# Two-level transfers for split blocks, doubled raw blocks, and biases asked for ahead, in a two-layer encoder

## The chip, the cores and the metric

The kernel runs on one core of a Trainium2 chip. The metric is the device time of one execution in microseconds (us); the median of several runs counts, and a profiled execution gives the trace. The engines are named as in the profile: PE (TensorE), DVE (VectorE), ACT (ScalarE), POOL (GpSimd) and SP (SyncE). SP, ACT and POOL issue transfers (DMAs), which 16 DMA engines of the core carry out.

## What is computed

Two layers of an encoder over 512 tokens of width 1024. Each has a feed-forward step, a mixer and a second feed-forward step; the mixer is what this case is about. The reference, cut to it:

```python
def reference(x, ...):
    for l in range(DEPTH):
        y = swiglu(rmsnorm(h, ffn1_pre_g[l]), ffn1_w_gu[l], ffn1_w_down[l])
        h = h + 0.5 * rmsnorm(y, ffn1_post_g[l])
        u = rmsnorm(h, mix_pre_g[l])
        proj = u @ w_in[l]
        qa, ka, va, qb, kb, vb, qc, kc, vc, gl = jnp.split(proj, split_at, axis=-1)
        oa = neighbourhood_attention(split_heads(qa, 8), split_heads(ka, 8), split_heads(va, 8), na_rpb[l])
        ob = sliding_window_attention(apply_rope(split_heads(qb, 8), cos, sin),
                                      apply_rope(split_heads(kb, 2), cos, sin),
                                      split_heads(vb, 2), sw_sink[l])
        ...   # qc, kc are turned by apply_rope too; two softmax maps per head
        oc = differential_attention(qc, kc, vc, lam, lam_init, diff_subln_g[l])
        ...
        yb = jnp.einsum('bsnc,ncd->bsnd', branches, w_branch[l])
        gates = jax.nn.sigmoid(gl.reshape(b, s, 3, D_MODEL) + b_gate[l])
        h = h + rmsnorm(jnp.sum(gates * yb, axis=2) @ w_out[l], mix_post_g[l])
        ...   # second feed-forward step

def apply_rope(t, cos, sin):
    t1, t2 = jnp.split(t, 2, axis=-1)
    return t * cos + jnp.concatenate([-t2, t1], axis=-1) * sin
```

The neighbourhood attention adds a bias to the scores, which is gathered from a small table `rpb` for each of 8 heads.

## The kernel before, in words

Every product is made of single-precision operands that are split in a high part `hi` and the rest `lo`, so that several fast matmuls give the exact product. A block is a tile of 128 rows (channels) and 512 columns (tokens), 262 KB.

**Projection** (`project`, one phase per layer). Column blocks of the projection (QA, KA, VA, QB, KB, VB, QC, KC, VC, then the gates from GL on) come out of PE, are evicted by ACT, and go to memory (DRAM) by POOL's queue. Blocks of queries and keys of branches A and B are split in `hi` and `lo` by `stacked` and stored as two tiles "part" by `store` (L1405). Blocks of QC and KC are stored as they are, as "raw", also by L1405; they are turned by the rotary step later, in the mixer.

**Mixer** (`mixer`). The string ORDER names its pieces in the order in which the code writes them: `qa`, `aa` (queries, keys, values of a pair of heads of branch A, and their attention), `kb`, `qb`, `ab` (branch B), `qc`, `ac`, `fc` (branch C), `ga` to `gc` (gates, 24 matmuls each, which fill PE between the attentions), `ya` to `yc` (the branches' output matmuls). A scheduler then orders each engine's instructions by its own costs, and each engine works its list strictly in order.

What a pair of heads needs is loaded by SP's queue. A *stack* `st` has 128 rows: 64 rows of `hi` over 64 rows of `lo` of the same head (or `lo` over `hi`), so that one matmul takes both. `restacked` fills each with two transfers of 64 rows (L1783, L1784) from the two "part" tiles. Blocks QA and KA (the first pair) stay on the chip. So the other three pairs of branch A load 6 stacks each (2 of the query block, 4 of the key block), and branch B loads 12: 30 stacks per layer. There are 14 buffers for them.

`rope` loads a raw block `x` (L1760) and a copy `sh` with its 32-row quarters exchanged in pairs (four transfers, L1768), and DVE then multiplies `x` by a table (L1769), `sh` by another (L1770) and adds (L1771). There are 8 such blocks per layer.

`ask` loads a head's raw biases `braw` (L1729) and has DVE form an edge tile and a middle tile `bedge`, `bmid` from them (L1744), in buffers of tag "g" (10 of them). `qkv_a` loads a pair's stacks and values first, and then asks for that pair's own biases.

The transfers of SP and ACT share eight completion semaphores in turn: a transfer that is given a semaphore waits, in its queue, until the one before it on that semaphore has landed.

Where a load's source is not a plain block, its access pattern is written out as a list of [pitch, count], outermost first. Before, that is so for the biases alone:

```python
    def raw_of(l, hd):
        return bass.AP(rpb.tensor, (l * 8 + hd) * 16 * RPBW, [[RPBW, 8], [1, 16], [1, 8 * RPBW]])
```

This is 8 runs of 16 rows of 512 numbers, laid into 128 rows of the tile.

Of the kernel before, what the change touches and what calls it, by code (L numbers as in the profile page):

```python
# [10 lines left out]
F32 = mybir.dt.float32  # L11
# [5 lines left out]
P = 128  # L17
# [3 lines left out]
T = 512  # L21
# [18 lines left out]
QA, KA, VA, QB, KB, VB, QC, KC, VC, GL = 0, 4, 8, 12, 16, 17, 18, 22, 26, 30  # L40
# [79 lines left out]
def encoder_kernel(ctx: ExitStack, tc: tile.TileContext, order, xT, wts, cols, rows, rpb, consts, tables, out):  # L120
    nc = tc.nc
# [5 lines left out]
    dr = ctx.enter_context(tc.tile_pool(name="dr", bufs=1, space=bass.MemoryType.DRAM))  # L127
# [19 lines left out]
    def nm(s):  # L147
        serial[0] += 1
        return f"{s}{serial[0]}"

    def big(tag, dt=F32, shape=(P, T), name="v"):
        if tag in BUFS:
            return sb.tile(list(shape), dt, tag=tag, name=nm(name), bufs=BUFS[tag])
        kind, pool = phase[0]
        return pool.tile(list(shape), dt, tag=tag, name=nm(name), bufs=ABUFS[kind][tag])
# [7 lines left out]
    V, A, G, PE = nc.vector, nc.scalar, nc.gpsimd, nc.tensor  # L163

    def f(t):
        return t.bitcast(F32)
# [94 lines left out]
    for l in range(L):  # L261
        for which in (1, 2):
            name = f"ffn{which}_w_down"
# [1104 lines left out]
    def project(l, op, accs):  # L1368
# [34 lines left out]
        def store(kind, x):  # L1403
            d = dr.tile([P, T], F32, tag=kind, name=nm(kind), bufs=60)
            G.dma_start(d, f(x))  # L1405
            return d

        def parts(x):
            hi, lo = big("t", F32R, name="hi"), big("t", F32R, name="lo")
            A.activation(hi, x, AF.Copy)  # L1410
            V.tensor_tensor(out=lo, in0=x, in1=f(hi), op=ALU.subtract)
            return hi, lo

        def stacked(c, x):
            hi, lo = parts(x)
            if c in (QA, KA):
                made[c] = []
                for s in range(2):
                    own, res = slice(64 * s, 64 * s + 64), []
                    for one, two in ((hi, lo), (lo, hi))[: 1 if c == QA else 2]:  # L1420
                        st = slots.pop(0)
                        nc.sync.dma_start(f(st)[0:64], f(one)[own])
                        nc.sync.dma_start(f(st)[64:128], f(two)[own])
                        res.append(st)
                    made[c].append((res + [None])[:2])
                return
            made[c] = store("part", hi), store("part", lo)

        def turned(c, x, heads):
            tp = bank("at")  # L1430
# [13 lines left out]
        turning, slowly, values = [], [], []  # L1444
# [5 lines left out]
        def turned_by(c, x):  # L1450
            sh = big("t", name="sh")
            for q in range(4):
                o = q ^ 1
                nc.sync.dma_start(sh[32 * q : 32 * q + 32], x[32 * o : 32 * o + 32])
            slowly.extend(
                (
                    lambda: V.tensor_tensor(out=x, in0=x, in1=turning[0], op=ALU.mult),
                    lambda: V.tensor_tensor(out=sh, in0=sh, in1=turning[1], op=ALU.mult),
                    lambda: V.tensor_tensor(out=x, in0=x, in1=sh, op=ALU.add),
                    lambda: stacked(c, x),  # L1460
                )
            )

        def ready(c, x):
            if c >= GL:
                gated(c, x)
            elif c < VA:
                stacked(c, x)
            elif QB <= c < VB:
                turned_by(c, x)  # L1470
            elif c < KB or c >= VB and (c < QC or c >= VC):
                values.append(lambda: turned(c, x, 1 if c >= VC else 2))
            else:
                made[c] = store("raw", x)

        def now():
            while values:
# [2 lines left out]
        def out(c, acc):  # L1480
            x = big("t", name="x")
            evict(x, c, acc)
            ready(c, x)
            now()

        made = {}
# [38 lines left out]
        for n, c0 in (("cosR", 0), ("sinR", 512)):  # L1525
            t = big("rr", name=n)
# [25 lines left out]
        def tables_of_a():  # L1552
            t = sb.tile([P, 4, T], F32, tag="n", name=nm("pre"), bufs=BUFS["n"])
            nc.sync.dma_start(t[:, 0, :], tables[:, 1024 : 1024 + 512])
            nc.sync.dma_start(t[:, 1, :256], tables[:, 1024 + 512 : 1024 + 768])
            for hd in range(2):
                nc.sync.dma_start(t[:, 2 + hd, :], raw_of(l, hd))
            made["tables"] = t
            made["edges"] = sb.tile([P, 4, T], F32, tag="n", name=nm("edges"), bufs=BUFS["n"])

        def gated(c, t):
            d = made["gates"][divmod(c - GL, KD)] = dr.tile([P, T], F32, tag="gate", name=nm("gate"), bufs=4 * KD)
            G.dma_start(d, t)
# [71 lines left out]
        work(len(slowly))  # L1635
        return made

    def raw_of(l, hd):
        return bass.AP(rpb.tensor, (l * 8 + hd) * 16 * RPBW, [[RPBW, 8], [1, 16], [1, 8 * RPBW]])

# [76 lines left out]
    def mixer(l, op, made):  # L1717
# [3 lines left out]
        for n in range(3):  # L1721
            masks[n] = pre[:, n // 2, 256 * (n % 2) : 256 * (n % 2) + 256]

        def ask(hd):
            if hd < 2:
                raws[hd] = pre[:, 2 + hd, :]
                return
            raw = raws[hd] = big("g", name="braw")
            nc.sync.dma_start(raw, raw_of(l, hd))  # L1729

        def biases(hd):
            raw = raws.pop(hd)
            if hd < 2:
                edge = made["edges"][:, hd, :]
                mid = made["edges"][:, 2, 2 * P * hd : 2 * P * (hd + 1)]
            else:
                edge = big("g", name="bedge")
                mid = big("g", shape=(P, 2 * P), name="bmid")

            def put(dst, mask, n0, n1):  # L1740

                src = raw[:, 7 * RPBW + 39 - 8 * n0 :]
                (ps0, pn), _ = src.ap
                V.tensor_tensor(  # L1744
                    out=dst.rearrange("p (d r c) -> p d r c", r=8, c=8),
                    in0=bass.AP(src.tensor, src.offset, [[ps0, pn], [-8, n1 - n0], [-RPBW, 8], [-1, 8]]),
                    in1=mask.rearrange("p (d r c) -> p d r c", r=8, c=8),
                    op=ALU.add,
                )

            put(edge[:, 0:256], masks[0], 0, 4)
            put(mid, masks[1], 0, 4)
            put(edge[:, 256:384], masks[2][:, :P], 2, 4)
            put(edge[:, 384:512], masks[2][:, P:], 0, 2)
            return lambda i: edge[:, 0:256] if i == 0 else edge[:, 256:512] if i == NT - 1 else mid


        def load(d, dt=F32, tag="tx"):
            x = big(tag, dt, name="x")
            nc.sync.dma_start(f(x), d)  # L1760
            return x

        def rope(c):
            x = load(made[c])
            sh = big("tx", name="sh")
            for q in range(4):
                o = q ^ 1
                nc.sync.dma_start(sh[32 * q : 32 * q + 32], made[c][32 * o : 32 * o + 32])  # L1768
            V.tensor_tensor(out=x, in0=x, in1=turning[0], op=ALU.mult)  # L1769
            V.tensor_tensor(out=sh, in0=sh, in1=turning[1], op=ALU.mult)  # L1770
            V.tensor_tensor(out=x, in0=x, in1=sh, op=ALU.add)  # L1771
            return x

        def restacked(c, both):
            if c in (QA, KA):
                return made[c]
            hi, lo = made[c]
            res = []
            for s in range(2):
                own, pair_ = slice(64 * s, 64 * s + 64), []  # L1780
                for one, two in ((hi, lo), (lo, hi))[: 2 if both else 1]:
                    st = big("st", F32R, name="st")
                    nc.sync.dma_start(f(st)[0:64], one[own])  # L1783
                    nc.sync.dma_start(f(st)[64:128], two[own])  # L1784
                    pair_.append(st)
                res.append((pair_ + [None])[:2])
            return res

        def values(c):
            t = made[c] if c == VA else [load(d, F32R, "st") for d in made[c]]  # L1790
            if c >= VC:
                return t
            v = [x.rearrange("p (b h d) -> p b h d", b=2, h=2) for x in t]
            return lambda j, s: v[j // 2][:, j % 2, s, :]
# [11 lines left out]


        def qkv_a(p):
            got = restacked(QA + p, False), restacked(KA + p, True), values(VA + p)
            for s in range(2):  # L1810
                ask(2 * p + s)
            return got

        oa = [sb.tile([P, 4, T], F32R, tag="X", name=nm("oa"), bufs=BUFS["X"]) for _ in range(2)]

# [121 lines left out]
        def qkv_b(c):  # L1937
            return restacked(c, c == KB)
# [69 lines left out]
        at = len(order) // HB  # L2008
# [62 lines left out]
    for l in range(L):  # L2071
        with open_phase("f"):
            X, accs = ffn(l, 1, X, accs)
        with open_phase("p"):
            made = project(l, X, accs)
# [63 lines left out]
```

## Time and profile before

| | |
|---|---|
| median of 3 runs | 2371.69 us (2371.62 to 2374.82) |
| profiled execution | 2370.88 us |
| its span, first to last instruction | 2369.1 us |
| mean granted PE clock | 0.996 |
| PE busy | 2342.6 us, 99% |
| DVE / ACT / POOL busy | 1892.4 / 1446.8 / 223.8 us |
| moved by DMA | 395.16 MB, mean 167 GB/s |
| stack loads `st<-part`, both layers | 120 of 128 KB |

The profile is read by views: the page with its table of engines; the waits, which give for each line the tile waited for, who made it, us in total, times, and the longest; the windows, which give for a stretch its length, then the busy time (and the instructions) of PE, PE's weight loads, DVE, ACT and POOL, then the granted PE clock as a share, the mean busy share of the 16 DMA engines, and GB/s; the timeline, with start, duration, engine, line, operation, tiles (out<-in), and in brackets the idle time before and what ended it; and the list of DMA issues, with count, KB each and the median us from issue to landing. Packets are the pieces in which the DMA engines move data; the profile counts them by size.

### The profile page before, as it was taken

Reading aid. Unit: us, or ns where it says so; the run is one execution under the profiler, and the core shown is the slowest. Engines: PE = TensorE matmul, PEld = TensorE weight load, DVE = VectorE, ACT = ScalarE, POOL = GpSimd, SP = SyncE. Lnnn points to the kernel's source line nnn. Section 1 sums busy time; section 2 is a strip of 40 time slices with the busy share of each in tenths; the row PEclk is TensorE's granted clock in tenths of the full one; section 3 lists DMA queues with packets and bytes.
Section 4 is the critical chain, followed back from the end, with each engine's and each line's share of the span. In section 5 each row is a group of like instructions: output and inputs, shape, how many; then the busy total and the mean of one; then the engine's idle time right before and its main releaser. Section 6 shows DMA issues by size and latency. Waiting matters only on the chain. (4 is left out here: it accounts for less than half of the span.)

```text
span 2369.1 us, 40269 instructions
## 1 busy us (share of the span) xinstructions
PE 2342.6 (99%) x15134; PEld 2109.5 (89%) x15134; DVE 1892.4 (80%) x3082; ACT 1446.8 (61%) x2715; POOL 223.8 (9%) x354
## 2 busy tenths in 40 slices
PE   9999999999999999999999999999999999999998
PEld 8999889997888889998899998889978788899987
DVE  7887988966888668888878878889579876788796
ACT  6555566667777465655655554666687764556563
POOL 0111001110121001110001110011101200011100
PEclk9999999999999999999999999999999999999999
DMA  5566446667565524664525565276774664256642
GB/s 170 162 169 190 154 145 187 207 219 207 168 174 189 167 97 147 166 162 165 175 87 168 162 178 196 102 216 199 222 206 139 195 206 140 97 147 172 190 148 84
DMA packets 138147, 395.16 MB, mean 167 GB/s; under 512 B 19296, under 2 KB 26080, under 8 KB 137440
## 3 DMA queue, kind: packets, MB, share of 16 engines
q1 hardware_dynamic: 102960, 260.37, 35.0%
q0 software_dynamic: 20160, 78.66, 12.4%
q10 hardware_dynamic: 14832, 53.56, 7.4%
q8 instruction: 119, 1.95, 0.3%
q14 instruction: 76, 0.62, 0.1%
HBM read 326.98 MB, written 80.74 MB: 172 GB/s over the span
## 5 line engine op out<-in xcount | busy, mean ns | idle before, releaser
L680 PE MATMUL mm<-X,h 128*128 128x256 f32 x1504 | 268.0, 278 | 1.2 <-DVE v L738 1.2
L680 PEld LDWEIGHTS mm<-X,h 128*128 128x128 f32 x1504 | 228.5, 188 | 2.5 <-DVE v L738 2.0
L225 DVE TENSOR_TENSOR w<-wr,w 128x512 fp32r<-128x512 f32 x264 | 178.9, 685 | 56.2 <-ACT w L224 55.2
L224 ACT ACTIVATE w<-wr 128x512 fp32r<-128x512 f32 x264 | 162.5, 627 | 96.4 <-PE mm L328 40.8
L326 PE MATMUL mm<-X,w 128*128 128x512 f32 (+1 forms) x570 | 218.3, 383 | 1.8 <-ACT X L553 1.8
L328 PE MATMUL mm<-X,w 128*128 128x512 f32 (+1 forms) x570 | 216.4, 380 | 0.8 <-DVE w L225 0.8
L327 PE MATMUL mm<-X,w 128*128 128x512 f32 (+1 forms) x570 | 216.2, 379 | 0.8 <-DVE X L554 0.7
L680 PE MATMUL mm<-ht,h 128*128 128x256 f32 x752 | 210.1, 279 | 0.0
L680 PE MATMUL mm<-ht,l 128*128 128x256 f32 x752 | 210.1, 279 | 0.0
L680 PE MATMUL mm<-lt,h 128*128 128x256 f32 x752 | 209.4, 278 | 0.0
L680 PE MATMUL mx<-ht,h 128*128 128x256 f32 x752 | 208.3, 277 | 0.6 <-ACT v L724 0.6
L680 PE MATMUL mm<-X,l 128*128 128x256 f32 x752 | 208.2, 277 | 0.0
L680 PE MATMUL mx<-ht,l 128*128 128x256 f32 x752 | 208.1, 277 | 0.0
L680 PE MATMUL mx<-lt,h 128*128 128x256 f32 x752 | 207.9, 277 | 0.0
L630 DVE TENSOR_TENSOR l<-wr,h 128x1024 fp32r<-128x1024 f32 x94 | 114.9, 1222 | 65.7 <-PE mm L680 65.7
L662 ACT ACTIVATE h<-wr 128x1024 fp32r<-128x1024 f32 x94 | 99.9, 1062 | 78.7 <-PE mx L680 55.5
L680 PE MATMUL at<-X,w 128*128 128x256 f32 x1128 | 144.2, 277 | 0.0
L680 PEld LDWEIGHTS mx<-ht,h 128*128 128x128 f32 x752 | 141.2, 188 | 1.4 <-ACT v L724 1.4
L680 PEld LDWEIGHTS mm<-ht,l 128*128 128x128 f32 x752 | 141.7, 188 | 0.1
L680 PEld LDWEIGHTS mm<-ht,h 128*128 128x128 f32 x752 | 141.7, 188 | 0.0
L680 PEld LDWEIGHTS mm<-lt,h 128*128 128x128 f32 x752 | 141.7, 188 | 0.0
L680 PEld LDWEIGHTS mx<-ht,l 128*128 128x128 f32 x752 | 141.2, 188 | 0.2 <-DVE l L640 0.2
(458 smaller groups left out, 6802.4 us busy)
## 6 DMA issues: line engine op xcount, KB each, us to landing
wr<-in_wts_dram SPq DMA_DIRECT2D x273, 512.0 KB, 4.6
wr<-in_wts_dram ACTq DMA_DIRECT2D x102, 512.0 KB, 4.1
sum<-in_wts_dram POOLq DMA_DIRECT2D x64, 512.0 KB, 5.3
st<-part SPq DMA_DIRECT2D x120, 128.0 KB, 5.1
ap<-in_wts_dram SPq DMA_DIRECT2D x20, 512.0 KB, 5.6
a<-kept SPq DMA_DIRECT2D x32, 256.0 KB, 6.3
ap<-sum SPq DMA_DIRECT2D x16, 512.0 KB, 4.3
x<-part SPq DMA_DIRECT2D x32, 256.0 KB, 3.8
```

The source lines that it names most:

```text
L224: A.activation(hi, raw, AF.Copy)
L225: V.tensor_tensor(out=lo, in0=raw, in1=f(hi), op=ALU.subtract)
L326: PE.matmul(acc, w[0], x[0], start=start, stop=False)
L327: PE.matmul(acc, w[0], x[1], start=False, stop=False)
L328: PE.matmul(acc, w[1], x[0], start=False, stop=stop)
L630: V.tensor_tensor(out=w["l1"], in0=self.raws[g][0], in1=f(w["h1"]), op=ALU.subtract)
L662: A.activation(self.W[g]["h24"], self.raws[g][1], AF.Copy)
L680: PE.matmul(acc, ws[i], xs[j], start=start and k == m == 0, stop=stop and k == n - 1 and m == 2, skip_group_check=True,)
```

## The change

Four edits, all in `project` and `mixer`, the same in both layers.

1. `stacked` stores `hi` and `lo` into one DRAM tile "both", one under the other, for key blocks whose stacks are needed in both orders `hi` once more as a third part. `restacked` loads each stack with one transfer instead of two.
2. A raw block is stored twice, by two transfers, so that its tile holds the upper 64 rows twice and then the lower 64 rows twice.
3. `rope` loads `x` from it, and the exchanged copy `sh` in one transfer instead of four.
4. `qkv_a` asks for biases ahead of its stacks: heads 0 to 3 with the first pair, 4 and 5 with the second, 6 and 7 with the third. The middle tiles of two heads share one buffer.

The function `halves(d, row)` names 64 rows from `row` and 64 rows from `row + 128` of a tile; as an access pattern that is 2 runs of 64 rows of 512 numbers.

```diff
--- before.py
+++ after.py
@@ -1424,7 +1424,11 @@
                         res.append(st)
                     made[c].append((res + [None])[:2])
                 return
-            made[c] = store("part", hi), store("part", lo)
+            n = 2 + (KA <= c < VA or c == KB)
+            d = dr.tile([n * P, T], F32, tag=f"both{n}", name=nm("both"), bufs=60)
+            for at, t in enumerate((hi, lo, hi)[:n]):
+                G.dma_start(d[P * at : P * at + P], f(t))
+            made[c] = d
 
         def turned(c, x, heads):
             tp = bank("at")
@@ -1471,7 +1475,9 @@
             elif c < KB or c >= VB and (c < QC or c >= VC):
                 values.append(lambda: turned(c, x, 1 if c >= VC else 2))
             else:
-                made[c] = store("raw", x)
+                made[c] = dr.tile([2 * P, T], F32, tag="raw", name=nm("raw"), bufs=60)
+                for n in range(2):
+                    G.dma_start(halves(made[c], 64 * n), f(x))
 
         def now():
             while values:
@@ -1635,6 +1641,10 @@
         work(len(slowly))
         return made
 
+    def halves(d, row):
+        pitch = d.ap[0][0]
+        return bass.AP(d.tensor, d.offset + row * pitch, [[P * pitch, 2], [pitch, 64], [1, T]])
+
     def raw_of(l, hd):
         return bass.AP(rpb.tensor, (l * 8 + hd) * 16 * RPBW, [[RPBW, 8], [1, 16], [1, 8 * RPBW]])
 
@@ -1721,6 +1731,8 @@
         for n in range(3):
             masks[n] = pre[:, n // 2, 256 * (n % 2) : 256 * (n % 2) + 256]
 
+        mids = []
+
         def ask(hd):
             if hd < 2:
                 raws[hd] = pre[:, 2 + hd, :]
@@ -1735,7 +1747,9 @@
                 mid = made["edges"][:, 2, 2 * P * hd : 2 * P * (hd + 1)]
             else:
                 edge = big("g", name="bedge")
-                mid = big("g", shape=(P, 2 * P), name="bmid")
+                if hd % 2 == 0:
+                    mids.append(big("g", name="bmid"))
+                mid = mids[-1][:, 2 * P * (hd % 2) : 2 * P * (hd % 2) + 2 * P]
 
             def put(dst, mask, n0, n1):
 
@@ -1761,11 +1775,9 @@
             return x
 
         def rope(c):
-            x = load(made[c])
+            x = load(halves(made[c], 0))
             sh = big("tx", name="sh")
-            for q in range(4):
-                o = q ^ 1
-                nc.sync.dma_start(sh[32 * q : 32 * q + 32], made[c][32 * o : 32 * o + 32])
+            nc.sync.dma_start(sh, halves(made[c], 32))
             V.tensor_tensor(out=x, in0=x, in1=turning[0], op=ALU.mult)
             V.tensor_tensor(out=sh, in0=sh, in1=turning[1], op=ALU.mult)
             V.tensor_tensor(out=x, in0=x, in1=sh, op=ALU.add)
@@ -1774,14 +1786,12 @@
         def restacked(c, both):
             if c in (QA, KA):
                 return made[c]
-            hi, lo = made[c]
             res = []
             for s in range(2):
-                own, pair_ = slice(64 * s, 64 * s + 64), []
-                for one, two in ((hi, lo), (lo, hi))[: 2 if both else 1]:
+                pair_ = []
+                for n in range(2 if both else 1):
                     st = big("st", F32R, name="st")
-                    nc.sync.dma_start(f(st)[0:64], one[own])
-                    nc.sync.dma_start(f(st)[64:128], two[own])
+                    nc.sync.dma_start(f(st), halves(made[c], P * n + 64 * s))
                     pair_.append(st)
                 res.append((pair_ + [None])[:2])
             return res
@@ -1806,10 +1816,9 @@
 
 
         def qkv_a(p):
-            got = restacked(QA + p, False), restacked(KA + p, True), values(VA + p)
-            for s in range(2):
-                ask(2 * p + s)
-            return got
+            for hd in ((0, 1, 2, 3), (4, 5), (6, 7), ())[p]:
+                ask(hd)
+            return restacked(QA + p, False), restacked(KA + p, True), values(VA + p)
 
         oa = [sb.tile([P, 4, T], F32R, tag="X", name=nm("oa"), bufs=BUFS["X"]) for _ in range(2)]
```

The first place in the order is SP's queue at the start of layer 0's mixer, just behind weight loads `wr`. `part` are the two stored parts of a block, `st` a stack, `x<-part` values, `braw` raw biases. Before:

```order
L211 DMA wr_5748<-in_wts_dram 128x1024
L1783 DMA st_5920<-part_4051 64x512
L1784 DMA st_5920<-part_4053 64x512
L1783 DMA st_5923<-part_4051 64x512
L1784 DMA st_5923<-part_4053 64x512
L1783 DMA st_5926<-part_4102 64x512
L1784 DMA st_5926<-part_4104 64x512
L1783 DMA st_5929<-part_4104 64x512
L1784 DMA st_5929<-part_4102 64x512
```

After, where `both` is the new tile:

```order
L211 DMA wr_5749<-in_wts_dram 128x1024
L1741 DMA braw_5921<-in_rpb_dram 128x1x512
L1741 DMA braw_5923<-in_rpb_dram 128x1x512
L1741 DMA braw_5925<-in_rpb_dram 128x1x512
L1741 DMA braw_5927<-in_rpb_dram 128x1x512
L1794 DMA st_5929<-both_4051 128x1x512
L1794 DMA st_5931<-both_4051 128x1x512
L1794 DMA st_5933<-both_4101 128x1x512
L1794 DMA st_5935<-both_4101 128x1x512
L1794 DMA st_5937<-both_4101 128x1x512
L1794 DMA st_5939<-both_4101 128x1x512
L1774 DMA x_5941<-part_4157 128x512
```

The four bias loads stand ahead of the first pair's stacks, and each stack is one row where it was two; a row of a stack now has the same form as a row of a bias load, 128x1x512.

The second place is POOL's queue in layer 0's projection, at the first raw blocks (`raw<-x` and `raw<-v`, from two buffers). Before:

```order
L1405 DMA part_5086<-hi_5082 128x512
L1405 DMA part_5088<-lo_5083 128x512
L1405 DMA raw_5146<-x_5060 128x512
L1405 DMA raw_5151<-v_4991 128x512
L1405 DMA part_5220<-hi_5216 128x512
L1405 DMA part_5222<-lo_5217 128x512
```

After:

```order
L1430 DMA both_5083<-hi_5079 128x512
L1430 DMA both_5083<-lo_5080 128x512
L1480 DMA raw_5142<-x_5057 2x64x512 x2
L1480 DMA raw_5148<-v_4988 2x64x512 x2
L1430 DMA both_5218<-hi_5214 128x512
L1430 DMA both_5218<-lo_5215 128x512
```

Each raw block is stored twice (x2), and its destination is written in 2 runs of 64 rows.

The third place is DVE's list in layer 0's branch A, where the rotary step of the first raw block stands. `bedge` and `bmid` are the bias tiles, `s,nmx` the scores of a head with their bias, `l` the sums of a softmax, `lo` the rest of a split block. Before:

```order
L1678 ISA s_6235,nmx_6234<-mx_6248,bedge_6228 128x256
L1678 ISA nmx_6234 128x1
L225 TENSOR_TENSOR w_6762<-wr_6760,w_6762 128x512
L1769 TENSOR_TENSOR x_7488<-x_7488,cosR_6548 128x512
L1692 RECIPROCAL l_6252<-l_6252 128x4
L353 TENSOR_TENSOR lo_6267<-at_6263,hi_6266 128x256
L1744 TENSOR_TENSOR bedge_6364<-braw_6147,pre_5225 128x256
L353 TENSOR_TENSOR lo_6276<-at_6272,hi_6275 128x256
L1744 TENSOR_TENSOR bmid_6365<-braw_6147,pre_5225 128x256
```

After:

```order
L353 TENSOR_TENSOR lo_6478<-at_6474,hi_6477 128x256
L1688 ISA s_6557,nmx_6556<-mx_6570,bedge_6550 128x256
L1688 ISA nmx_6556 128x1
L353 TENSOR_TENSOR lo_6487<-at_6483,hi_6486 128x256
L1781 TENSOR_TENSOR x_7456<-x_7456,cosR_6529 128x512
L1782 TENSOR_TENSOR sh_7458<-sh_7458,sinR_6531 128x512
L1702 RECIPROCAL l_6574<-l_6574 128x4
L1783 TENSOR_TENSOR x_7456<-x_7456,sh_7458 128x512
```

Before, the multiplication L1769 stood alone between the last scores of head 3 and the reciprocal of its sums (L1692); after, the same multiplication is L1781, it stands behind scores of a later head (`mx_6570`), and the multiplication of `sh` (L1782) and the sum (L1783) follow it.

## The prediction

> **What bounds the kernel now.** I read the page's table of engines first, then the waits of TensorE, then those of VectorE, then windows of the two places where TensorE loses time.
>
> ```profile
> PE 2342.6 (99%) x15134; PEld 2109.5 (89%) x15134; DVE 1892.4 (80%) x3082; ACT 1446.8 (61%) x2715; POOL 223.8 (9%) x354
> PE o L1710 <- DVE lo L353: 6.9, 2, 3.7
> DVE x L1769 <- DMA x<-raw: 11.4, 3, 5.6
> 550.00:560.00 10.00, 6.33 (x30) 5.09 (x31) 3.00 (x11) 5.76 (x19) 0.00 (x0) 0.83 1.00 247
> 560.00:570.00 10.00, 10.00 (x50) 8.42 (x49) 5.94 (x23) 6.24 (x19) 0.00 (x0) 0.83 0.66 176
> 1720.00:1730.00 10.00, 6.79 (x39) 5.42 (x38) 4.87 (x20) 5.92 (x20) 0.00 (x0) 1.00 1.02 223
> 1730.00:1740.00 10.00, 10.00 (x50) 8.42 (x51) 5.57 (x21) 7.20 (x22) 0.00 (x0) 0.83 0.85 194
> ```
>
> TensorE is busy 99% of the span: it is the bound, and only its own waits can be won back. Its largest wait, 6.9 us in two pieces, is for `lo` of the attention, once in each layer's branch A. The window rows place them at 550 to 560 and 1720 to 1730: TensorE is busy 6.33 and 6.79 us of 10 there (3.7 and 3.2 us lost), and in three of the four rows the granted clock is 0.83 of full speed (1.7 us of work lost in each). That is 12 us for both layers.
>
> The timeline of VectorE, ScalarE and TensorE shows the cause in layer 0:
>
> ```profile
> 556.73 0.69 DVE L1769 TENSOR_TENSOR x<-x,cosR 128x512 f32<-128x512 f32 x1 [5.60 <-DMA x<-raw]
> 557.34 0.17 DVE L1692 RECIPROCAL l<-l 128x4 f32<-128x4 f32 x1
> 557.43 0.39 DVE L353 TENSOR_TENSOR lo<-at,hi 128x256 fp32r<-128x256 f32 x1
> 557.87 0.58 PE L1710 MATMUL o<-lo,x 128*128 128x256 f32 x1 [3.67 <-DVE lo L353]
> ```
>
> VectorE stands 5.60 us in the rotary step of a raw block, whose load has not landed. Behind it, in VectorE's order, stand the reciprocal and the split `lo` that TensorE waits for. The load is late because the transfers of that stretch fill the queues (share 1.00 and 1.02 above).
>
> **The change, what it takes away.** In the new order of VectorE the rotary multiplication stands after the scores of three more heads, together with its two companions, so a late load no longer stands ahead of those heads' `lo`. So the 12 us can go. SP issues 60 stack transfers and 48 shifted ones fewer, at about 0.5 us each 54 us of SP over the run; SP only issues, and TensorE never waits for its issue time as such. POOL gets 12 stores more per layer, at 0.54 us each (row below) 6.5 us; it is busy 9% of the span and waits 433.3 us for `hi`, so the issues lie in that waiting. Their bytes (about 3 MB per layer, against 395 MB in all) I cost at nothing, up to 1 us per layer. The biases: the first four heads' are asked for ahead of the stacks, two heads share one middle buffer; VectorE's bias additions are the same in number. Nothing to half a microsecond, either way.
>
> ```profile
> POOL part L1405 <- ACT hi L1410: 433.3, 24, 152.1
> 458.67 0.54 POOL L1405 DMA_DIRECT2D raw<-x  x1 [3.48 <-ACT x L1398]
> 501.13 0.54 POOL L1405 DMA_DIRECT2D raw<-v  x1
> ```
>
> **What it adds: how a transfer is spread over the engines.** Every new transfer has a side written as 2 runs of 64 rows, outermost dimension 2. No transfer before has that. The nearest is the load of the raw biases, written as 8 runs of 16 rows. How many of the 16 DMA engines does that one use? First the count of packets, the list of issues (first and last of its 49 rows, and the two that load the biases), then windows.
>
> ```profile
> DMA packets 138147, 395.16 MB, mean 167 GB/s; under 512 B 19296, under 2 KB 26080, under 8 KB 137440
> wr<-in_wts_dram SPq DMA_DIRECT2D x273, 512.0 KB, 4.6
> ...
> braw<-in_rpb_dram SPq DMA_DIRECT2D x12, 256.0 KB
> ...
> pre<-in_rpb_dram SPq DMA_DIRECT2D x4, 256.0 KB
> ...
> colt<-in_cols_dram ACTq DMA_DIRECT2D x1, 73.0 KB
> ```
>
> The 49 rows add up to 1214 transfers. If each closed with 16 small packets, one for every engine, there would be 19424 under 512 bytes. There are 19296: 128 fewer, exactly 8 for each of the 16 transfers (12 and 4) that are written as 8 runs. The windows say the same in another way:
>
> ```profile
> 560.01 1.37 SPq L1729 DMA_DIRECT2D braw<-in_rpb_dram  x2
> 561.43 2.30 SPq L1768 DMA_DIRECT2D sh<-raw  x4
> 566.71 0.50 SPq L1783 DMA_DIRECT2D st<-part  x1
> 565.00:566.00 1.00, 1.00 (x10) 0.95 (x9) 1.00 (x5) 0.32 (x2) 0.00 (x0) 1.00 0.53 164
> 566.00:566.60 0.60, 0.60 (x6) 0.56 (x6) 0.08 (x2) 0.60 (x2) 0.00 (x0) 1.00 0.48 143
> 457.00:458.00 1.00, 1.00 (x11) 1.00 (x10) 1.00 (x3) 0.02 (x2) 0.00 (x0) 1.00 0.78 320
> ```
>
> Two bias loads and four small ones are issued from 560.01, nothing more from SP until 566.71. At the tail of these the DMA share is 0.53 and 0.48: half the engines work, though two bias loads are behind one another. So eight engines serve such a load, and the same eight serve both. I take it that the outermost dimension sets the number, and that 2 runs of 64 give **two engines, the same two each time**.
>
> The Trainium skill's page "DMA: Bandwidth & Descriptors", section "Why a DMA increments its semaphore by 16 and not by 1", states such a rule: the largest number up to 16 that divides the slowest dimension of both sides, and for SP and ACT the lowest-numbered engines. For 8 runs the trace agrees (128 packets, share 0.48 to 0.53); no run here shows 2 runs.
>
> **The price.** A busy engine moved 164 / (0.53 x 16) = 19.3 GB/s in the half-share window and 320 / (0.78 x 16) = 25.6 in the fast one at 457. I take 22, between them, since two engines alone leave the memory lightly loaded. A transfer of 262 KB is 131 KB per engine: 6.0 us (5.1 to 6.8), where 16 engines need a sixteenth of the bytes each, 0.7 us.
>
> ```profile
> st<-part SPq DMA_DIRECT2D x120, 128.0 KB, 5.1
> x<-raw SPq DMA_DIRECT2D x16, 256.0 KB, 3.2
> sh<-raw SPq DMA_DIRECT2D x64, 64.0 KB, 2.0
> 516.27 0.44 SPq L1783 DMA_DIRECT2D st<-part  x1
> ...
> 714.58 1.70 SPq L1768 DMA_DIRECT2D sh<-raw  x4
> 510.00:720.00 210.00, 205.53 (x1105) 173.16 (x1103) 162.38 (x459) 155.48 (x392) 30.74 (x57) 0.98 0.66 187
> 1682.00:1892.00 210.00, 204.75 (x1103) 172.20 (x1103) 162.33 (x459) 154.91 (x391) 30.63 (x57) 0.99 0.67 187
> ```
>
> Per layer there become of these 30 stacks, 8 raw blocks and 8 shifted ones: 46 transfers of 262 KB, nearly all issued within the 210 us from 510 to 720 (the bulk of the stacks from 516.27, the last shifted block at 714.58; layer 1 alike). On two engines: 46 x 6.0 = 276 us. The stretch moves 187 GB/s x 210 us = 39.3 MB; less the 12.1 MB of the 46 that leaves 27.2 MB, a sixteenth of it, 1.7 MB, through each engine: 77 us. The two engines need **353 us for what the stretch does in 210**. Each of the 46 is read by TensorE or VectorE within that stretch, so it grows by about 143 us per layer, 286 in all. The 12 us of the old stall lie within the 210 and are not taken off again.
>
> The first 60 us tell the same sooner: branch A's 18 stacks, one raw and one shifted block are 20 x 6.0 = 120 us of the two engines, before anything else. New waits follow at the scores (L1685) for `st`: behind a late stack stand, on TensorE, the scores and gate matmuls ordered after it; on SP, its next loads, weights too, which share the two engines' queue.
>
> Fast end: 5.1 us each and 66 us beside them make 301, or 91 per layer; some 15 us more could be won by stacks asked for earlier (in before one was issued at 495). That is 76 x 2 = 152: 2523. Slow end: 6.8 and 88 make 401, 191 per layer: 2753.
>
> POOL's doubled raw stores are written 2 by 64 too: 16 per layer from 458.67 to 501.13, two engines each. If these pairs change from store to store, nothing of it reaches the path. If they are again the same two, 16 x 6.0 = 96 us of work falls into about 50 us that also have 20 us of other traffic, and up to 66 us per layer are pushed on. No row tells; I take nothing and keep 132 us as the upper end.
>
> The Trainium skill, same page and section, gives POOL's transfers engines in turn from a moving cursor; by it the price here is nothing. No run here shows it.
>
> **The rivals.** (a) *The pairs of runs are flattened or spread over all 16 engines.* Then only the recovery is left: the rotary step leaves the middle of branch A, and the stretch's queues (share 1.00) give back up to 3 us. 2370.9 - 12 + 3 = 2362, faster. For it: both sides have 128 rows; against it: so has the bias load. It decides when the share during stack loads is 0.6 or more. (b) *Two engines, but another pair for each transfer.* Throughput is kept, each landing is some 5 us later; a margin of 2 to 4 us is overrun once or twice a layer: 2370.9 - 12 + 2 x 5 = 2369. Against it: the two bias loads on the same half. (c) *The POOL stores crowd the same two engines*: 2657 + up to 132, about 2790 at full price. (d) *The change does not move the rotary step*: ruled out by the order; without its recovery (a) would be 2371.
>
> **How the numbers follow.** The sum goes by the profiled execution, 2370.88 us (span 2369.1), 0.8 below the median 2371.69. 2370.9 + 286 = 2657 us. Chances: forecast 0.75, (a) 0.08, (b) 0.05, (c) 0.12. The range takes in the forecast's price bounds and (c) nearly whole: 2520 to 2800; left out are (a) and (b) and a tail. Faster by over 0.2%: (a) and a little of (b), 0.09; within 0.2% (about what a measurement of this kernel can tell from no change): the most of (b), 0.04; slower: 0.87.
>
> **What would show it.** Right: long DMA times at `st<-both` (tens of us from issue to landing), a DMA share in branch A near 2 engines in 16 while SP's stack loads are the only ones, TensorE waiting at L1685 for `st` in every pair, some 100 us per layer in A and B and the rest at the rotary steps, and 16216 packets under 512 bytes (1130 transfers x 16, less the 128, less 14 for each of the 92 loads and 32 stores with 2 runs); the rest of the kernel unchanged. Wrong: `st<-both` landing in 5 us with a share near 1.00, which is (a), or in 8 us at full throughput, (b); or the loss sitting in the projection, (c).

## The result, and the profile after

| | before | after |
|---|---|---|
| median | 2371.65 us (4 runs, 2366.04 to 2374.82) | 2742.97 us (4 runs, 2740.09 to 2745.06) |
| ratio to before | | 1.1571, 95% interval 1.1548 to 1.1595 |
| span of the profiled execution | 2369.1 us | 2739.3 us |
| mean granted PE clock | 0.996 | 0.938 |

The changed kernel is 371 us slower. The page after, the engine table and the count of packets:

```profile
PE 2420.4 (88%) x15134; PEld 2164.5 (79%) x15134; DVE 1902.6 (69%) x3082; ACT 1452.0 (53%) x2715; POOL 243.8 (9%) x378
DMA packets 151387, 401.55 MB, mean 147 GB/s; under 512 B 31001, under 2 KB 37785, under 8 KB 150681
```

TensorE is no longer the bound: it stands still for 12% of the span. Of the 370 us by which the profiled span is longer, 292 are TensorE standing still (318.9 us after, 26.5 before). The other 78 are its busy time: the same 15134 matmuls take 2420.4 us instead of 2342.6, at a mean granted clock of 0.938 instead of 0.996. The waits of TensorE and of VectorE (us in total, times, the longest):

```profile
PE mx L1685 <- DMA st<-both: 157.1, 20, 18.2
PE o L1901 <- DVE lo L353: 33.3, 4, 9.7
PE mx L680 <- ACT v L724: 27.2, 4, 8.0
DVE sh L1782 <- DMA sh<-raw: 86.7, 15, 8.6
```

The scores of branches A and B wait for stacks. Branch C waits for the splits of VectorE, which itself stands 86.7 us before exchanged raw blocks. A third wait, `mx L680` for ACT, belongs to the projection.

Then SP's timeline in layer 0's branch A, and three windows of it:

```profile
541.00 26.01 SPq L1794 DMA_DIRECT2D st<-both  x6
567.12 6.42 SPq L1774 DMA_DIRECT2D x<-part  x2
573.63 2.01 SPq L1741 DMA_DIRECT2D braw<-in_rpb_dram  x2
575.74 30.22 SPq L1794 DMA_DIRECT2D st<-both  x6
617.00:622.00 5.00, 2.10 (x16) 1.82 (x15) 1.43 (x5) 1.21 (x6) 0.00 (x0) 1.00 0.13 49
642.00:647.00 5.00, 4.07 (x18) 3.88 (x19) 1.74 (x7) 1.06 (x3) 0.00 (x0) 0.58 0.13 48
541.00:777.00 236.00, 137.22 (x647) 114.55 (x646) 97.59 (x307) 97.08 (x271) 10.70 (x21) 0.77 0.32 102
```

The window of 5 us at 617 is the clearest line of this case. The share of the 16 DMA engines is 0.13, which is two of sixteen, and 49 GB/s are moved: 24.5 GB/s for each of the two. A stack of 262 KB takes 262 / 49 = 5.35 us. TensorE works 2.10 of these 5 us. SP's rows show the same from the queue's side: six issues stretch over 26 and 30 us, and a single one takes 5.14 us by the median of all 60 (0.50 for a half stack, `st<-part`, before). So not only the transfers queue; SP itself is held in issuing them, and values and biases stand behind. The windows also show the clock: it is 0.58 at 642 and 0.77 over branches A and B.

Where the 370 us lie, read from the starts of TensorE's matmuls in the timeline (first and last score of branches A and B, last output matmul of branch C):

| stretch | before, L0 / L1 | after, L0 / L1 | longer |
|---|---|---|---|
| up to the first score | 516.6 / from L0's end 916.1 | 539.0 / 938.9 | 22.4 / 22.8 |
| branches A and B | 130.2 / 128.8 | 238.0 / 238.7 | 107.8 / 109.9 |
| branch C | 126.1 / 127.6 | 180.7 / 181.3 | 54.6 / 53.7 |

The rest of the kernel is as long as before.

### The profile page after: what moved, and what is told of

Its sections match the earlier page's. It is cut to its first block, busy times and chain, and to the rows that moved or that the text cites. A ratio compares the mean times of both kernels' runs of the same rounds, so it can differ in the third digit from the quotient of the medians.

```text
span 2739.3 us, 40123 instructions
## 1 busy us (share of the span) xinstructions
PE 2420.4 (88%) x15134; PEld 2164.5 (79%) x15134; DVE 1902.6 (69%) x3082; ACT 1452.0 (53%) x2715; POOL 243.8 (9%) x378
## 2 busy tenths in 40 slices
DMA packets 151387, 401.55 MB, mean 147 GB/s; under 512 B 31001, under 2 KB 37785, under 8 KB 150681
## 5 line engine op out<-in xcount | busy, mean ns | idle before, releaser
L680 PE MATMUL mm<-X,h 128*128 128x256 f32 x1504 | 268.2, 278 | 2.0 <-DVE v L738 1.9
L680 PE MATMUL mx<-ht,h 128*128 128x256 f32 x752 | 211.4, 281 | 27.5 <-ACT v L724 27.2
L680 PEld LDWEIGHTS mm<-X,h 128*128 128x128 f32 x1504 | 228.5, 188 | 3.6 <-DVE v L738 3.0
L326 PE MATMUL mm<-X,w 128*128 128x512 f32 (+1 forms) x570 | 226.3, 397 | 2.6 <-ACT X L553 1.8
L327 PE MATMUL mm<-X,w 128*128 128x512 f32 (+1 forms) x570 | 223.0, 391 | 0.8 <-DVE X L554 0.7
L328 PE MATMUL mm<-X,w 128*128 128x512 f32 (+1 forms) x570 | 221.7, 389 | 0.0
L1685 PE MATMUL mx<-st,st 128*128 128x256 f32 (+1 forms) x224 | 63.7, 377 | 175.2 <-DMA st<-both 157.1
L680 PE MATMUL mm<-ht,h 128*128 128x256 f32 x752 | 211.2, 281 | 6.0 <-ACT at L719 6.0
L680 PE MATMUL mx<-lt,h 128*128 128x256 f32 x752 | 210.5, 280 | 0.0
L680 PE MATMUL mx<-ht,l 128*128 128x256 f32 x752 | 210.5, 280 | 0.0
L680 PE MATMUL mm<-ht,l 128*128 128x256 f32 x752 | 210.5, 280 | 0.0
L680 PE MATMUL mm<-lt,h 128*128 128x256 f32 x752 | 209.8, 279 | 0.0
L680 PE MATMUL mm<-X,l 128*128 128x256 f32 x752 | 208.2, 277 | 0.0
L1685 PEld LDWEIGHTS mx<-st,st 128*128 128x128 f32 x224 | 45.0, 234 | 186.6 <-DMA st<-both 95.8
L680 PEld LDWEIGHTS mx<-ht,h 128*128 128x128 f32 x752 | 143.8, 191 | 28.6 <-ACT v L724 28.6
L352 ACT ACTIVATE hi<-at 128x256 fp32r<-128x256 f32 (+2 forms) x160 | 70.8, 444 | 163.4 <-PE at L1716 38.4
L353 DVE TENSOR_TENSOR lo<-at,hi 128x256 fp32r<-128x256 f32 (+2 forms) x160 | 79.4, 500 | 104.4 <-PE o L1720 81.8
L680 PEld LDWEIGHTS mm<-ht,h 128*128 128x128 f32 x752 | 142.0, 189 | 7.2 <-ACT at L719 7.2
L621 DVE TENSOR_TENSOR r<-wr,wr 128x1024 f32<-128x1024 f32 x94 | 115.0, 1224 | 46.4 <-DMA wr<-in_wts_dram 40.3
```

Source lines behind the costliest of these rows:

```text
L326: PE.matmul(acc, w[0], x[0], start=start, stop=False)
L327: PE.matmul(acc, w[0], x[1], start=False, stop=False)
L328: PE.matmul(acc, w[1], x[0], start=False, stop=stop)
L352: A.activation(hi, src, AF.Copy)
L353: V.tensor_tensor(out=lo, in0=src, in1=f(hi), op=ALU.subtract)
L621: V.tensor_tensor(out=w["r13"], in0=base, in1=r[0], op=ALU.add)
```

## The experiments

**One part mended at a time.** Four kernels, each the changed one with some edits; their diffs are cut to the changed lines. In the first, a stack's source is named by its 64 rows first and its two halves inside. Rows of queries and keys are permuted alike, so the sums over them stay the same.

```diff
+    def woven(d, row):
+        return bass.AP(d.tensor, d.offset + row * pitch, [[pitch, 64], [P * pitch, 2], [1, T]])
-                    nc.sync.dma_start(f(st), halves(made[c], P * n + 64 * s))
+                    nc.sync.dma_start(f(st), woven(made[c], P * n + 64 * s))
```

> The changed kernel with one edit: a stack's transfer names 64 rows outermost and the two halves inside (64 x 2 x 512) instead of 2 runs of 64 rows; same bytes, same count, same order; the rows of query and key stacks are permuted alike, so the products are the same. Raw blocks stay as in the change. Theory (the outermost dimension sets how many DMA engines serve a transfer): the 108 and 110 us of the branches A and B go, the rest stays, 2743 - 218 = 2525 us, 2490 to 2560; no TensorE wait for a stack over 2 us; packets under 512 bytes rise by 60 x 14 = 840. Rival (a transfer of 262 KB with a source in two levels is slow to issue whatever stands outermost): 2743, 2720 to 2760.

Measured: 2513.24 us (1.0611, interval 1.0586 to 1.0636). Branches A and B take 121.5 and 122.2 us, the two-engine queue is gone from them, and the waits for stacks are no longer among TensorE's first:

```profile
PE o L1905 <- DVE lo L353: 33.7, 5, 9.9
PE mx L680 <- ACT v L724: 25.1, 5, 6.6
DMA packets 152226, 401.55 MB, mean 160 GB/s; under 512 B 31840, under 2 KB 38624, under 8 KB 151520
```

Small packets rose by 839, where 840 were expected. Bytes, counts and queue order were left alone, so the order of the dimensions in the access pattern is the cause of the loss in A and B, not the size of the transfer or its two levels.

The second leaves the stacks as in the change and takes the raw blocks back to the plain store and loads of before.

```diff
-                made[c] = dr.tile([2 * P, T], F32, tag="raw", name=nm("raw"), bufs=60)
-                for n in range(2):
-                    G.dma_start(halves(made[c], 64 * n), f(x))
+                made[c] = store("raw", x)
-            x = load(halves(made[c], 0))
-            nc.sync.dma_start(sh, halves(made[c], 32))
+            x = load(made[c])
+            for q in range(4):
+                o = q ^ 1
+                nc.sync.dma_start(sh[32 * q : 32 * q + 32], made[c][32 * o : 32 * o + 32])
```

> The changed kernel with the raw blocks as before (one plain store, one plain load, four loads of 32 rows); stacks by 2 runs of 64 rows, biases as in the change. Theory: only branches A and B lose, the projection's 22 us and branch C's 54 us per layer go: 2743 - 154 = 2589, 2560 to 2610; first score of the mixer back at 516 us. Rival (the loss of branch C and of the projection is carried over from the stacks): 2650 to 2743.

Measured: 2574.46 us (1.0871, 1.0848 to 1.0893). The first score is back at 516.5, and branch C takes 134.7 us instead of 180.7; A and B still take 224.5 and 223.1 us. The losses of the projection and of branch C therefore come from the raw blocks alone.

The third has both edits.

> The changed kernel with the stacks by 64 rows outermost and the raw blocks as before: what is left of the change is one transfer per stack, the joint tile, and the biases asked for ahead. Theory: the loss is gone and the old stall at the rotary step as well: 2371.7 - 12 + up to 3, 2355 to 2368. Rival (the order of the work, biases first and rope late, costs of its own): 2375 to 2400. Rival (two levels are slow as such): 2590 or more.

Measured: 2367.64 us (0.9997, 0.9984 to 1.001). The loss is gone whole. The time lies within the expected range, but the gain that was expected beside it was not found; more on that below. Layer 0's branches A and B take 119.4 us here and branch C 134.9, where before had 130.2 and 126.1: the new order moves some 35 gate matmuls from the one to the other. So, against this kernel, the change cost 118.6 us in A and B and 45.8 in C, the same sum as in the table but for 2 us.

The fourth is stacks_by_row with plain stores of the raw blocks.

```diff
-                for n in range(2):
-                    G.dma_start(halves(made[c], 64 * n), f(x))
+                for n in range(4):
+                    G.dma_start(made[c][64 * n : 64 * n + 64], f(x)[64 * (n // 2) : 64 * (n // 2) + 64])
```

> As stacks_by_row, and each raw block is stored by four plain transfers of 64 rows instead of two with 2 runs of 64 rows; twice as many stores on POOL, the same bytes; loads of the raw blocks stay at 2 runs. Theory (the doubled stores take few engines for long and hold up the weight loads of the projection): the projection's 22 us per layer go, 45 us less than stacks_by_row, 2460 to 2500; stores land in 3 to 5 us. Rival (the added bytes and issues are what costs): not less than stacks_by_row, up to 20 us more.

Measured: 2482.53 us (1.0483, 1.0463 to 1.0503), 31 us less than stacks_by_row where 45 were expected: the first score comes at 520.5 instead of 538.1, not quite at the 515.5 of both_mended, and branches A and B take 3 to 5 us longer in each layer. The list of issues shows what the stores did, with the median us to landing at the end of each row. First the changed kernel:

```profile
raw<-x POOLq DMA_DIRECT2D x16, 256.0 KB, 11.6
raw<-v POOLq DMA_DIRECT2D x16, 256.0 KB, 13.9
```

and of plain_stores:

```profile
raw<-x POOLq DMA_DIRECT2D x32, 128.0 KB, 4.0
raw<-v POOLq DMA_DIRECT2D x32, 128.0 KB, 4.4
```

Twice as many stores of the same bytes land three times as soon. What lay on TensorE's path were the weights of the projection: in the changed kernel ScalarE waits longer for them (waits of ACT up to the first score, before and then after)

```profile
ACT w L650 <- DMA wr<-in_wts_dram: 7.7, 7, 1.5
ACT w L224 <- DMA wr<-in_wts_dram: 1.9, 2, 1.4
```

```profile
ACT w L650 <- DMA wr<-in_wts_dram: 16.1, 7, 6.6
ACT w L224 <- DMA wr<-in_wts_dram: 14.1, 2, 7.7
```

**The dose.** If the outermost dimension sets the number of engines, 4 and 8 runs must lie between 2 and 64.

```diff
-        return bass.AP(d.tensor, d.offset + row * pitch, [[pitch, 64], [P * pitch, 2], [1, T]])
+        return bass.AP(d.tensor, d.offset + row * pitch, [[64 * pitch, 4], [pitch, 32], [1, T]])
-                    nc.sync.dma_start(f(st), woven(made[c], P * n + 64 * s))
+                    nc.sync.dma_start(f(st), woven(made[c], 0))
```

For 8 runs the first line is `[[32 * pitch, 8], [pitch, 16], [1, T]]`.

> As both_mended, but each stack's source is written as 4 runs of 32 rows (outermost dimension 4). The stacks hold other rows of the same tile than they should, so the output is not the reference's; bytes, counts and order are those of both_mended and raw_as_before. Theory: four engines, 131/2 KB each, some 2.9 us of them per stack where two engines took 5.1 to 5.7. 18 stacks are 52 us within the first 45 to 60 us of branch A, all 30 are 87 us: a loss of 0 to 20 us per layer against both_mended, 2366 to 2408; 18464 - 60 x 12 = 17744 packets under 512 bytes. Rival (any source in gapped runs costs what raw_as_before does): 2560 to 2590.

> As outer_four with 8 runs of 16 rows; again the stacks hold other rows. Theory: eight engines, 1.5 us per stack, 27 us in branch A: within 3 us of both_mended, 2364 to 2372; 18464 - 60 x 8 = 17984 packets under 512 bytes. Rival: 2560 or more.

| outermost | kernel | median us | ratio to before | A and B, L0 | packets under 512 B |
|---|---|---|---|---|---|
| 2 | raw_as_before | 2574.46 | 1.0871 (1.0848 to 1.0893) | 224.5 us | 17624 |
| 4 | outer_four | 2442.01 | 1.0305 (1.0283 to 1.0327) | 154.6 us | 17744 |
| 8 | outer_eight | 2387.90 | 1.0083 (1.0058 to 1.0109) | 130.5 us | 17984 |
| 64 | both_mended | 2367.64 | 0.9997 (0.9984 to 1.001) | 119.4 us | 18464 |

The packet counts are the expected ones to the last packet: each of the 60 stacks leaves 2, 4, 8 or 16. The times fall with the dose, but both kernels are slower than expected (by 34 us over the upper end, and by 16). SP's rows for the first six stacks, of raw_as_before, outer_four and outer_eight in this order:

```profile
518.33 26.16 SPq L1794 DMA_DIRECT2D st<-both  x6
```

```profile
517.72 12.69 SPq L1798 DMA_DIRECT2D st<-both  x6
```

```profile
517.48 8.03 SPq L1798 DMA_DIRECT2D st<-both  x6
```

These rows run from the first issue to the end of the last, with waits between. A single issue takes, by the median of all 60, 5.10, 2.00 and 0.58 us, and 0.55 in both_mended: SP issues to eight engines as fast as to sixteen. What I had left out, as I read it, is that the load has to be met at deadlines, not on average: the first stacks and values are asked for within a few microseconds, and values and other loads stand behind the stacks. No run tries this by itself. With eight runs TensorE waits no longer for a stack but for values behind the stacks, which is 10.3 of the 20 us over both_mended:

```profile
PE mx L1687 <- DMA x<-part: 10.3, 2, 5.4
```

**Nothing on few engines.** plain_stores with plain loads as well.

```diff
-            x = load(halves(made[c], 0))
+            x = big("tx")
-            nc.sync.dma_start(sh, halves(made[c], 32))
+            for n in range(2):
+                nc.sync.dma_start(x[64 * n : 64 * n + 64], made[c][P * n : P * n + 64])
+            for n in range(2):
+                nc.sync.dma_start(sh[64 * n : 64 * n + 64], made[c][P * n + 32 : P * n + 96])
```

> As plain_stores, and the loads of the raw blocks too are plain: x and the exchanged copy by two transfers of 64 rows each. So nothing but the bias loads uses fewer than 16 engines. Theory: branch C's 47 us per layer go: 2482.5 - 94 = 2388 or less; what is left over both_mended (2367.6) is the cost of the doubled stores, which showed as 5 us per layer at the first score of plain_stores: 2368 to 2380. Rival (branch C loses by the new place of the rotary step): 2440 or more.

Measured: 2383.06 us (1.0049, 1.0031 to 1.0067), 3 us over the upper end. Branch C is back at 133.6 us, so its loss came from the loads. The first score comes at 520.1 and A and B take 124.7 us instead of 119.4, much as in plain_stores, whose raw loads are written otherwise; so I put both to the doubled stores, which the two kernels share, and this is argued, not shown. In A and B TensorE waits for stacks again:

```profile
PE mx L1689 <- DMA st<-both: 9.9, 6, 3.0
```

How stores of the projection come to delay these stacks was not tried. Two transfers for the exchange, where before had four, win nothing that pays for the bytes.

**The edits alone.**

> The kernel before with only the edit of the biases (asked for ahead, two middles in a buffer). Theory: this edit moves the rotary step out of the middle of branch A by itself, so the 3.7 and 3.4 us waits there go, and small waits of 0.8 to 1.2 us take part of it back as in both_mended: 2364 to 2371. Rival (the joint stack transfers were needed for that, since SP issues twice as many): no change at the old stall, 2370 to 2376.

> The kernel before with only the joint tile and one transfer per stack, its source named by 64 rows outermost; biases and raw blocks as before. Theory: 16 engines serve each stack, SP issues 60 transfers fewer, and the rotary step leaves the middle of branch A here too, with the biases still asked for pair by pair: the two waits of 3.7 and 3.4 us go, smaller ones take part of it back: 2361 to 2369 where before is 2370. Rival (the joint tiles' 1.05 MB more stores per layer hold up the projection or branch A as the doubled raw stores did): 2370 to 2378.

> The same kernel as both_mended, in more rounds, beside stacks_alone. Theory: 4 us of idle TensorE less in its profile than before: 0.997 to 0.999 of before. Rival (nothing is won): 0.999 to 1.001.

Each was put into the kernel before, the stacks in the form with 64 rows outermost. Measured: biases_alone 2373.79 us (1.0024, 1.0011 to 1.0038), stacks_alone 2372.74 us (1.0032, 1.0019 to 1.0045), both together, in more rounds, 2368.56 us (1.0006, 0.9996 to 1.0017). In all three the old stall at `lo` is gone, and none is faster than before. All three gains that were expected failed to come: biases_alone and stacks_alone are each some 6 us slower than the kernel before in the same session (2368.16 and 2366.69 us), and both together are as fast. The waits of TensorE in biases_alone and in stacks_alone show what stands there instead:

```profile
PE mx L1675 <- DMA st<-part: 5.8, 2, 3.5
```

```profile
PE o L1717 <- ACT hi L352: 4.8, 2, 2.4
PE o L1718 <- DVE lo L353: 2.2, 4, 1.0
```

No version beats the kernel before. Why the two edits cost something each by itself and nothing together was not tried.

## Why the prediction was right, and where it was off

The measured 2743 us lie within the range and 86 above the forecast of 2657: 40 of the 86 lie in the branches A to C, 45 in the projection, for which I had added nothing. For branches A and B the mechanism was the forecast one; for branch C and the projection it was not in full, and the sizes were off.

**Two engines, the same two.** Right, and shown: the share of 0.13 while only stacks are loaded, 24.5 GB/s per engine, 26 and 30 us for six issues, the packet counts of four kernels, and the loss that goes when only the order of the dimensions changes. The rule of the Trainium skill's page "DMA: Bandwidth & Descriptors" (section "Why a DMA increments its semaphore by 16 and not by 1") held for 2, 4, 8 and 64 on SP's queue; rival (a), all 16 engines, falls, and so does (b), other pairs each time, since the share stays at 0.13 while several stacks are issued one behind another. Which two of the 16 they are, no view shows.

**The size for branches A to C.** I took 6.0 us per transfer and a stretch that the two engines fill: 143 us longer per layer. It came out 162.4 and 163.6, and that the forecast came so near is partly luck, from two errors of opposite sign. The price was too high: it was 5.35 us, and at 24.5 GB/s my own sum would have been 46 x 5.35 + 69 = 315 us for 210, 105 longer. And the stretch is not filled evenly. In A and B it is: 36 transfers of 5.35 us are 193, and the other traffic of the window 541 to 777 (102 GB/s x 236 us = 24.1 MB, less 9.4, a sixteenth of it at 24.5 GB/s) is 37; together 230 of 236 us, a queue that is full. In branch C it is not: 10 transfers are 54 us, with some 57 for other traffic (137 GB/s x 181 us, less 2.6 MB), 110 of 181 us. Yet C grew by 54 us (46 against both_mended), because there the length of a single transfer counts: VectorE needs `x`, then `sh`, both from the same two engines, one behind the other. Its rows in branch C:

```profile
822.42 0.69 DVE L1781 TENSOR_TENSOR x<-x,cosR 128x512 f32<-128x512 f32 x1 [1.99 <-DMA x<-raw]
830.10 0.69 DVE L1782 TENSOR_TENSOR sh<-sh,sinR 128x512 f32<-128x512 f32 x1 [6.39 <-DMA sh<-raw]
```

And the clock was not in my sum:

```profile
777.00:958.00 181.00, 146.54 (x653) 116.73 (x652) 108.64 (x242) 92.76 (x187) 21.79 (x42) 0.89 0.45 137
```

In both_mended as many matmuls keep TensorE busy for 134.8 us of branch C, at a clock of 1.00. So some 34 of the 46 us are TensorE standing still and 12 its lower clock. The step that failed is "the two engines need 353 us for what the stretch does in 210": a sum of work bounds a queue that is full, and says too little of a chain that waits for each link.

**POOL's stores.** I took nothing and kept 66 us per layer as the upper end. That term was mis-sized: the projection became 22.4 and 22.8 us longer, and in layer 0 17.6 of these go when the same bytes are stored by plain transfers (first score at 520.5 instead of 538.1). It is rival (c) in kind, but its mechanism is not shown. The stores do not all crowd the same two engines: four of them, issued from 458.64 to 461.09, land 10.1 to 14.4 us after their issue, which is 1.05 MB in at most 16.9 us, or 62 GB/s, where two engines moved 49 for SP. In two windows of the changed kernel while they are in flight, no packet of a weight load runs, and the share is well above 0.13:

```profile
461.00:463.00 2.00, 2.00 (x19) 2.00 (x19) 2.00 (x3) 1.35 (x3) 0.89 (x2) 1.00 0.32 48
463.00:465.00 2.00, 2.00 (x20) 2.00 (x19) 2.00 (x4) 0.15 (x1) 0.59 (x1) 1.00 0.35 52
```

Pairs in turn would fit this share; the Trainium skill's moving cursor (same page and section) would give that. But 48 and 52 GB/s at a share of five engines are no more than two engines moved for SP, so each store is slow by itself; its form makes it so (plain_stores), by what mechanism no run shows. By "if these pairs change from store to store, nothing of it reaches the path" I had left out that a late store can reach TensorE by way of ScalarE's waits for weights: up to the first score they are 30.2 us (16.1 and 14.1 above), where before they were 9.6.

One sign that I had named did not come: 16216 packets under 512 bytes, where 31001 were counted. SP's loads left what I expected (839 of 840 in stacks_by_row, and the whole dose); POOL's stores did not, as the last section shows.

**The 12 us of the old stall.** That they lie within the stretch and are not taken off was harmless here. As a gain they were mis-sized. In both_mended the two waits of 3.84 and 3.37 us between TensorE's matmuls are gone. But the time from one matmul's start to the next, less the usual one (the median for its shape), summed over the run, fell by 4.3 us only (from 61.1 to 56.8): waits of 0.8 and 1.2 us and many smaller ones took their place in branch A. The spans of the two profiled executions differ by 4.0 us (2369.1 and 2365.1). And 5.1 of the 12 us were clock, 1.7 in each of three windows. The profile that I read them from has a mean clock of 0.996; of 42 executions of the kernel before that were timed with the experiments, 7 have 0.996 (median 2372.6 us) and 35 have 0.997 to 0.999 (median 2366.7 us). So most executions do not seem to lose these 5 us in the first place; since only one was profiled, this is not shown. The times of both_mended show no gain that can be measured.

**The rest.** Not every new transfer has 2 runs, as I wrote: the stores of `both` are plain. Stores and bytes were costed at nothing to 1 us per layer. Even with plain transfers the doubled raw blocks cost 5 us per layer in the projection (first score 520.1 against 515.5); whether by POOL's issues or by the bytes was not separated.

The biases asked for ahead cost nothing together with the joint stacks. Alone they cost 5.6 us, about the 5.8 us that TensorE then waits for stacks, ahead of which the bias loads stand in SP's queue; that these are the cause is argued, not shown. The joint stacks alone cost 6.0 us, for which the record has no cause.

## What to carry to other kernels

Merging transfers is not free of what the merged pattern looks like: put a dimension that 16 divides outermost (here 64 rows first and the halves inside, with the operands permuted alike; 2, 4 and 8 outermost were served by as many engines), and look at the DMA share when such a transfer is alone. Count small packets before and after: for SP's loads they told how many engines served a transfer without a single timing (for POOL's stores in two runs they did not). Waits came with a lower clock here, too: the mean granted clock was 0.938 in the kernel of 2743 us, 0.963 in that of 2574, 0.984 in that of 2442 and 0.996 in that of 2388. And a stall need not be worth its length: of 12 us some 4 came back in the profile here and none in the times, and smaller waits took its place.

## What the runs showed of the hardware that was not expected

SP is held while it issues to a queue whose engines are behind: a stack's issue took 0.5 to 10.5 us, by the median 5.14 (541.00 above, six in 26.01 us), where a half stack's before took 0.44 us (516.27 in the prediction) and by the median 0.50. So every other load of that queue is late too, at a DMA share of 0.13. And POOL's stores in two runs left many more packets than SP's loads in two runs: after has 31001 under 512 bytes, where 1130 transfers with 16 each, less 128 for the bias loads and less 92 x 14 for SP's two-run loads, are 16664; the rest is 448 for each of the 32 stores, but for one packet. With plain stores of the same bytes (plain_stores) they are gone: 18016 are counted, and 1162 x 16, less 128, less 32 x 14, are 18016. What these packets are was not tried.
